# A new order of work at the two attention-to-MLP joints of a two-layer float32r transformer block

## The chip, the cores and the metric

One core of one Trainium2 chip runs the whole program. The metric is device time in microseconds. An engine name stands for: PE the matmul engine, DVE the vector engine, ACT the scalar engine, POOL the GpSimd engine, SP the engine that here only issues transfers. Each engine works through its own queue in order.

## The reference, cut to what matters

Batch 1, 256 latent tokens, 256 context tokens, width 1024, two layers. Layer 0 mixes latents and context by retention and passes both through an MLP; layer 1 lets the latents attend to a neighbourhood and to the context, and passes the latents alone through its MLP.

```python
for i in range(DEPTH):                      # DEPTH = 2
    h = x * (1.0 + sc1) + sh1
    hc = ctx * (1.0 + sc1c) + sh1c
    y, yc = mixer(h, hc, ...)               # retention (i = 0), neighbourhood attention (i = 1)
    x = layer_norm(ALPHA * x + g1 * y, ln_g[i, 0], ln_b[i, 0])
    h = x * (1.0 + sc2) + sh2
    x = layer_norm(ALPHA * x + g2 * sq_relu_mlp(h, w1[i], w2[i]), ln_g[i, 1], ln_b[i, 1])
    if not last:                            # the same for ctx with yc and the context's modulation
        ...
def sq_relu_mlp(h, w1, w2):
    return jnp.square(jax.nn.relu(h @ w1)) @ w2
```

A joint is the stretch between the last products of a mixer's output projection and the first products of the MLP: residual add, layer norm, transposition, modulation, and then `h @ w1`.

## The kernel before

Every float32 operand of a product is split in two float32r parts: `hi` is ACT's cast of it, `lo` is DVE's (or POOL's) subtraction of `hi` from it. A product a*b is three matmuls: ah*bh, ah*bl, al*bh. A weight tile comes by one transfer of 512 KB into one of four `raw` buffers; `fetch` issues the transfer and ACT's cast to `hi` and puts the subtraction on a list; `lows(n)` runs the first n of that list; `take(n, ahead, open_)` fetches and subtracts until enough units are there and hands out n of them (`open_` units may still lack their `lo`). `hi` and `lo` have five buffers each; a `raw` buffer is free again when its `lo` is made, so a late `lo` is a late transfer four units further on.

A scheduler puts all instructions into the engines' queues by their order in the program and by when it reckons their operands ready. An engine wrapper with `.on = True` pins an instruction behind the one traced just before it on that engine; instructions that aren't pinned may still be put ahead of pinned ones.

Layer 0's joint. Four token tiles t of 128 (0 and 1 are latents, 2 and 3 context). `proj` makes a tile's output projection, `add_to` adds it to the residual `R`, `stat` and `moments` give mean and `rstd` (the power is POOL's), `shift_of` makes `nmr`, `white` is the normalized tile `xn`, `turn` transposes it on PE into two PSUM tiles `pt`, `affine` modulates these to `aff` (half 0 on DVE, half 1 on ACT), `mod_split` makes `hTh` (ACT) and `hTl`. The MLP's first weight columns come in units of 512 x 256; two units make a pair, called `us[0:2]` and `us[2:4]` for the first two pairs. `mm1` multiplies a pair by the columns `LAT` (256 latents, matmuls 256 wide), `CTX` (256 context columns) or `ALL` (512 wide) into two PSUM banks; both column ranges of a pair share the banks. `evac1` takes a bank out by `relu_sq`: Relu on ACT, the square `r<-p,r` on DVE, a cast on ACT, a subtraction on DVE. The latents' products of the two pairs run while tiles 2 and 3 are made ready; the context's products follow, once the latents' part of the same bank is out.

Layer 1's joint. Two latent tiles. Output-projection weights come in eight units; the last two for half 1 lie in a slot (`hilo`) and in scratch tiles (two 512-column pieces). `attend(n)` ends with `rt`, `oTh`, `oTl` of head group n. `settle_last` adds a half of a tile to `R`, `center` makes `x0` and `x1`, `mod_pt` turns them (`pts0`, `pts1`), `affine_half` modulates tile 0, `direct` tile 1, `tok_part` are the first MLP products in token-major form, `turn_block` transposes their activations into `hid`. `settle_quarter` adds tile 1's second half in two quarters. The opening is the first pass of the loop over `f4`, `f2` that follows: `f4 == 1 and f2 == 0`. I number the MLP's weight units of this layer u0, u1, ...: each `f2` uses two of them (the opening u4 and u5, the next u6 and u7, then u8 and u9, and so on).

PE, ACT and DVE are pinned through both joints; POOL is pinned in the second half of layer 1's; SP is not pinned.

Of the kernel before, what the change touches and what calls it, by code (L numbers as in the profile page):

```python
# [10 lines left out]
F32 = mybir.dt.float32  # L11
F32R = mybir.dt.float32r
AF = mybir.ActivationFunctionType
# [91 lines left out]
def kernel(  # L105
# [171 lines left out]
    def lows(n=100):  # L277
        for lo, raw, hi in pending[:n]:
            dve.tensor_sub(out=lo, in0=raw, in1=hi.bitcast(F32))
        del pending[:n]  # L280
# [366 lines left out]
    def mod_split(tmp, half, t, eng, halves=False):  # L647
        ks = slice(4 * half, 4 * half + 4)
        if halves:
            hi, lo = (  # L650
                h[:, ks, :NLAT].rearrange("p k (b r) -> p k b r", b=2)[:, :, :, 64 * t : 64 * t + 64]
                for h in (hTh, hTl)
            )
            split(tmp[:].rearrange("p (k b r) -> p k b r", k=4, b=2), hi, lo, eng)
            return
        split(tmp[:].rearrange("p (k t) -> p k t", k=4), hTh[:, ks, tsl(t)], hTl[:, ks, tsl(t)], eng)

# [412 lines left out]
    for h in range(RH):  # L1070
# [159 lines left out]
        else:  # L1230
# [14 lines left out]
            def white(t, mv, r):  # L1245
                act.activation(out=xns[t], in_=R[t], func=AF.Identity, scale=r[:], bias=shift_of(mv, r)[:])
# [4 lines left out]
            def affine(t, pts):  # L1251
                return [mod_aff(pts[half], half, t, A, B) for half in range(2)]
# [12 lines left out]
            white(0, *m0)  # L1265
# [8 lines left out]
            white(1, *m1)  # L1274
# [12 lines left out]
            white(2, *m2)  # L1287
# [27 lines left out]

    G2 = None
    for hf in range(2):
# [9 lines left out]
        if hf == 0:  # L1327
            us = take(2, 2)
            pbs = [[bank("p1") for _ in range(2)] for _ in range(2)]
            hts = [hslot(fp) for fp in range(2)]  # L1330
            mm1(us, LAT, pbs[0], range(0, 4))
            take(0, 1)
            f2 = affine(2, turn(2))
            white(3, *m3)
            mm1(us, LAT, pbs[0], range(4, KC))
            us += take(2, 2)
            for half in range(2):
                mod_split(f2[half], half, 2, dve)
            mm1(us[2:4], LAT, pbs[1], range(0, 4))
            p3 = turn(3)  # L1340
            mm1(us[2:4], LAT, pbs[1], range(4, KC))
            f3 = affine(3, p3)
            take(0, 1)
            for half in range(2):
                mod_split(f3[half], half, 3, dve)
            for fp in range(2):
                evac1(pbs[fp], LAT, hts[fp])
            for e in ORDER:
                e.on = False
            for fp in range(2):  # L1350
                mm1(us[2 * fp : 2 * fp + 2], CTX, pbs[fp])
                evac1(pbs[fp], CTX, hts[fp])
            hid += hts
            outside()
# [532 lines left out]
    add_to(1, 0, t01[0], dve)  # L1887
    invert(n)
    gather(n)
    attend(n - 1)  # L1890
    flip(n)
    turned(n)
    lows(1)
    fetch(1, at=N_V)
    lows(1)
    fetch(1, True)

    us = take(4, 0, 2)
# [7 lines left out]
    def wo_last(t, half, cols=slice(0, 512)):  # L1906
        ps = wops[half, t, cols.start] if half else bank("pnw")
        mmo(ps, t, (4, 5, 6, 7), us[2 * half : 2 * half + 2], cols, start=half == 0)
        return ps
# [32 lines left out]
    fetch(1)  # L1942
# [9 lines left out]
    us4 = take(2, 0)  # L1952
# [65 lines left out]
    lo0 = [affine_half(pts0, half, 0, True, (dve, pool)[half]) for half in range(2)]  # L2018
# [3 lines left out]
    lo0[0]()  # L2022
# [5 lines left out]
    lo0[1]()  # L2028
# [194 lines left out]
```

## Time and profile before

| what | us |
|---|---|
| median of 3 runs | 1208.73 (1206.9 to 1209.21) |
| the profiled execution | 1205.15 |
| its span, first to last instruction | 1203.4 |
| layer 0's joint in the span | about 436 to 484 |
| layer 1's joint in the span | about 986 to 1056 |

All instructions issued through the wrappers carry one line (L84) in the profile, so a group is known by its names: `lo<-raw,hi` is a weight's subtraction, `hi<-raw` its cast, `hTl<-aff,hTh` a tile's low part. In a row of the timeline the columns are start, length (of the whole group, where `xN` tells of N alike), engine, line, operation, output and inputs, shape, count; a bracket tells how long the engine sat idle before it and what ended that.

### The profile page before, as it was taken

What the parts mean: (1) busy time and instruction counts of PE and PEld (TensorE: products, weight loads), DVE (VectorE), ACT (ScalarE), POOL (GpSimd) and SP (SyncE); (2) the same over time, 40 slices, a digit from 0 to 9 for tenths busy, and PEclk for the clock granted to TensorE, in tenths of its full rate; (3) what the DMA queues carried; (4) which work ended last, traced back from release to release, by engine and by line L of the source; (5) the groups of instructions that cost most, each with busy time, mean ns of one, the idle gap of its engine ahead of it and who ended that gap; (6) DMA issues with size and microseconds to landing.
All of it is one profiled execution on the core that took longest, in us unless ns stands there. A gap on an engine that the chain in (4) does not pass through costs nothing.

```text
span 1203.4 us, 17830 instructions
## 1 busy us (share of the span) xinstructions
PE 1176.1 (98%) x6867; PEld 986.4 (82%) x6867; DVE 825.5 (69%) x1307; ACT 477.8 (40%) x809; POOL 255.0 (21%) x390
## 2 busy tenths in 40 slices
PE   7999899999999999999999999999999999999997
PEld 5777788788878888888888888889778878999886
DVE  3778676768576478667876675578576688787445
ACT  3562122323222246442122333227466665666341
POOL 1103400420340131491203000122444431000001
PEclk9999999999999999999999999999999999999999
DMA  9766443344143123856566655546244335566660
GB/s 302 225 228 193 144 134 107 105 133 165 62 154 117 59 82 117 263 113 195 170 197 204 211 189 196 185 150 204 80 144 133 103 115 162 182 211 202 236 210 36
DMA packets 130265, 193.16 MB, mean 161 GB/s; under 512 B 9676, under 2 KB 73332, under 8 KB 130180
## 3 DMA queue, kind: packets, MB, share of 16 engines
q1 hardware_dynamic: 121796, 179.02, 46.1%
q0 software_dynamic: 7232, 10.44, 3.9%
q10 hardware_dynamic: 1152, 2.56, 0.7%
q8 instruction: 54, 0.88, 0.3%
q14 instruction: 31, 0.25, 0.1%
HBM read 187.15 MB, written 5.75 MB: 160 GB/s over the span
## 4 chain that ended last, share of the span: by engine, by line
PE 82%; DVE 8%; DMA 4%; issue 2%; ACT 2%; POOL 1%; SPq 0%; DVEq 0%; ACTq 0%; POOLq 0%
PE p L84 40%; PE pq L84 7%; PE pv L84 7%; PE pn L84 5%; PE pg L84 5%; PE pw L84 4%; PE pnv L84 4%; DMA rawa<-in_ada_w_dram 2%; DVE lo L84 2%; PE po L84 2%; PE ppt L84 2%; PE pS L84 1%; PE pqk L84 1%; PE pada L84 1%; PE pav L84 1%
## 5 line engine op out<-in xcount | busy, mean ns | idle before, releaser
L84 ACT CAST hi<-raw 128x1024 fp32r<-128x1024 f32 (+2 forms) x228 | 231.9, 1032 | 323.6 <-PE p L84 123.4
L84 DVE TENSOR_TENSOR lo<-raw,hi 128x1024 fp32r<-128x1024 f32 (+2 forms) x228 | 274.0, 1214 | 109.5 <-ACT hi L84 109.1
L84 PE MATMUL p<-hi,hid 128*128 128x512 f32 (+1 forms) x832 | 241.8, 374 | 0.0
L84 PEld LDWEIGHTS p<-hi,hid 128*128 128x128 f32 x832 | 152.2, 188 | 27.7
L84 PE MATMUL p<-hTh,lo 128*128 128x256 f32 (+1 forms) x512 | 167.5, 327 | 1.9 <-DVE lo L84 1.9
L84 PE MATMUL p<-hTh,hi 128*128 128x256 f32 (+1 forms) x512 | 167.9, 328 | 0.2 <-ACT hTh L84 0.2
L84 PE MATMUL p<-hTl,hi 128*128 128x256 f32 (+1 forms) x512 | 167.3, 327 | 0.4 <-DVE hTl L84 0.4
L84 PE MATMUL p<-lo,hid 128*128 128x512 f32 (+1 forms) x416 | 155.3, 373 | 0.0
L84 DVE SCALAR_TENSOR_TENSOR acc<-rawa,scol,acc 128x1024 f32<-128x1024 f32 x56 | 74.7, 1344 | 66.0 <-DMA rawa<-in_ada_w_dram 66.0
L84 POOL TENSOR_TENSOR R<-R,acc 128x512 f32<-128x512 f32 x40 | 63.2, 1596 | 209.9 <-DVE acc L84 209.8
L84 PEld LDWEIGHTS p<-hTh,lo 128*128 128x128 f32 x512 | 96.4, 188 | 11.2 <-DVE lo L84 2.5
L84 PEld LDWEIGHTS p<-hTl,hi 128*128 128x128 f32 x512 | 96.4, 188 | 9.5 <-DVE hTl L84 0.8
L84 PEld LDWEIGHTS p<-hTh,hi 128*128 128x128 f32 x512 | 96.3, 188 | 9.2 <-ACT hTh L84 0.4
L84 PEld LDWEIGHTS p<-lo,hid 128*128 128x128 f32 x416 | 78.4, 188 | 13.6
L84 ACT CAST hid<-r 128x256 fp32r<-128x256 f32 (+1 forms) x64 | 32.0, 500 | 109.9 <-DVE r L84 109.9
L84 DVE SCALAR_TENSOR_TENSOR strips<-rawa,scol,strips 128x512 f32<-128x512 f32 x84 | 66.8, 830 | 9.8 <-DMA rawa<-in_ada_w_dram 9.7
L84 POOL TENSOR_TENSOR rstd<-rstd,misc 128x1 f32<-128x1 f32 x28 | 18.8, 672 | 208.5 <-DVE rstd L84 207.2
L84 PE MATMUL pw<-hi,ol 128*128 128x512 f32 x128 | 51.0, 398 | 6.5 <-DVE ol L84 6.5
L84 ACT ACTIVATE s<-s,mn 128x512 f32<-128x512 f32 x64 | 45.5, 713 | 26.2 <-DVE mn L84 26.2
L84 PE MATMUL pw<-hi,oh 128*128 128x512 f32 x128 | 51.6, 403 | 0.0
L84 PE MATMUL pg<-hi,hTh 128*128 128x512 f32 x128 | 51.3, 401 | 0.0
L84 PE MATMUL pw<-lo,oh 128*128 128x512 f32 x128 | 50.5, 394 | 0.0
(238 smaller groups left out, 2288.3 us busy)
## 6 DMA issues: line engine op xcount, KB each, us to landing
raw<-in_mlp_w_dram SPq DMA_DIRECT2D x128, 512.0 KB, 4.5
rawa<-in_ada_w_dram SPq DMA_DIRECT2D x80, 512.0 KB, 3.9
raw<-in_ret_w_in_dram SPq DMA_DIRECT2D x42, 512.0 KB, 3.5
raw<-in_nat_w_in_dram SPq DMA_DIRECT2D x24, 512.0 KB, 5.1
rawq<-in_ada_w_dram SPq DMA_DIRECT2D x16, 512.0 KB, 6.4
raw<-in_ret_w_o_dram SPq DMA_DIRECT2D x16, 512.0 KB, 3.5
bias<-rpb_rows POOLq DMA_DIRECT2D x32, 128.0 KB, 2.9
raw<-in_nat_w_o_dram SPq DMA_DIRECT2D x8, 512.0 KB, 4.2
```

The costliest lines, as they stand in the source:

```text
L84: r = f(*args, **kwargs)
```

## The change

Layer 0's joint. One more weight unit is fetched ahead of tile 2's `white`. The shift of tile 3 is made ahead of tile 2's `affine`, and tile 3's `white` stands between the casts of tile 2's halves. The low parts of a tile are separated from its casts (`mod_high` returns the subtraction, to be run later), half 1 first. The context's products run in a new function `ctx_mm1`: all high-by-high products of both banks first, then the two others, and k from 4 to 7 ahead of 0 to 3; PE stays pinned through them.

Layer 1's joint. `invert` of the last head group moves behind `attend` of the one before, the residual's add of t01 behind `flip`; the scratch unit is fetched behind the last `attend`, one of its two subtractions goes to POOL; tile (0, half 1)'s products run as `wo_parts`, the products with the weights' low parts last; one MLP unit is fetched two steps earlier; both low parts of tile 0 go to POOL (one was DVE's); the first products of the second hidden block are split in two; in the opening, a fetch and its subtraction follow each of the two evacuations, and the transposed activations go between them.

```diff
+    def mod_high(tmp, half, t):
+        ...
+        act.copy(out=hi, in_=raw)
+        return lambda: dve.tensor_sub(out=lo, in0=raw, in1=hi.bitcast(F32))
...
             take(0, 2)
-            white(2, *m2)
+            fetch(1)
+            white(2, shift_of(*m2), m2[1])
...
+    def ctx_mm1(us, pb):
+        for i in range(2):
+            for k in (4, 5, 6, 7, 0, 1, 2, 3):
+                pe.matmul(
+                    pb[i][:, CTX], lhsT=us[k // 4][0][:, k % 4, tsl(i)], rhs=hTh[:, k, CTX],
+                    start=k == 4, stop=False,
+                )
+        for i in range(2):
+            for k in (4, 5, 6, 7, 0, 1, 2, 3):
+                wh, wl = (w[:, k % 4, tsl(i)] for w in us[k // 4])
+                pe.matmul(pb[i][:, CTX], lhsT=wl, rhs=hTh[:, k, CTX], start=False, stop=False)
+                pe.matmul(pb[i][:, CTX], lhsT=wh, rhs=hTl[:, k, CTX], start=False, stop=k == 3)
...
-            us = take(2, 2)
+            us = take(2, 2, 1)
...
             mm1(us, LAT, pbs[0], range(0, 4))
-            take(0, 1)
+            lows(1)
+            shift = shift_of(*m3)
             f2 = affine(2, turn(2))
-            white(3, *m3)
+            fetch(1)
+            low21 = mod_high(f2[1], 1, 2)
+            white(3, shift, m3[1])
+            low20 = mod_high(f2[0], 0, 2)
             mm1(us, LAT, pbs[0], range(4, KC))
+            lows(1)
+            low21()
             us += take(2, 2)
-            for half in range(2):
-                mod_split(f2[half], half, 2, dve)
             mm1(us[2:4], LAT, pbs[1], range(0, 4))
             p3 = turn(3)
             mm1(us[2:4], LAT, pbs[1], range(4, KC))
             f3 = affine(3, p3)
+            low20()
+            low31, low30 = (mod_high(f3[half], half, 3) for half in (1, 0))
+            low31()
+            low30()
             take(0, 1)
-            for half in range(2):
-                mod_split(f3[half], half, 3, dve)
             for fp in range(2):
                 evac1(pbs[fp], LAT, hts[fp])
-            for e in ORDER:
+            for e in ORDER[1:]:
                 e.on = False
             for fp in range(2):
-                mm1(us[2 * fp : 2 * fp + 2], CTX, pbs[fp])
+                ctx_mm1(us[2 * fp : 2 * fp + 2], pbs[fp])
                 evac1(pbs[fp], CTX, hts[fp])
+            pe.on = False
...
     wo_first(1, 0)
-    add_to(1, 0, t01[0], dve)
-    invert(n)
     gather(n)
     attend(n - 1)
+    invert(n)
     flip(n)
     turned(n)
     lows(1)
+    add_to(1, 0, t01[0], dve)
     fetch(1, at=N_V)
-    lows(1)
-    fetch(1, True)
-
-    us = take(4, 0, 2)
+    us = take(2, 0)
...
     attend(n)
+    lows(1)
+    fetch(1, True)
     mmo(ps, 0, (6, 7), us[0:2], start=False, k0=4)
-    lows(2)
+    lows(1, pool)
+    lows(1)
+    us += take(2, 0)
+    settle_last(0, 0, ps)
     fetch(1)
-    settle_last(0, 0, ps)
     lows(1)
-    settle_last(0, 1, wo_last(0, 1))
+    settle_last(0, 1, wo_parts(0, 1))
     mv0, r0 = moments(0)
     wo_first(1, 1, HALVES)
+    fetch(1)
...
-    fetch(1)
+    us4 = take(2, 0, 1)
     lows(1)
     settle_last(1, 0, wo_last(1, 0))
...
-    lo0 = [affine_half(pts0, half, 0, True, (dve, pool)[half]) for half in range(2)]
+    lo0 = [affine_half(pts0, half, 0, True, pool) for half in range(2)]
+    for low in lo0:
+        low()
     ps = [wo_last(1, 1, cols) for cols in HALVES]
     for q in range(2):
         stat_quarter1(q)
-    lo0[0]()
     settle_quarter(2, ps[0])
     settle_quarter(3, ps[1])
...
-    lo0[1]()
...
     tok_part(p00, 0, 0, *HL, LOW)
+    tok_part(p00, 0, 0, *LH, LOW)
     tok_part(p00, 0, 0, *HH, HIGH)
     tok_part(p00, 0, 0, *HL, HIGH)
-    tok_part(p00, 0, 0, *LH, LOW)
-    tok_part(p01, 0, 1, *HH, start=True)
+    tok_part(p01, 0, 1, *HH, LOW, start=True)
     tok_part(p01, 0, 1, *LH, LOW)
     tok_part(p00, 0, 0, *LH, HIGH, stop=True)
+    tok_part(p01, 0, 1, *HH, HIGH)
...
             mm1(us, LAT, pb, at=AT)
-            if opening:
-                turn_block(r10, 1, 0)
-                turn_block(r11, 1, 1)
-                for e in (pe, act, dve, pool):
-                    e.on = False
             dve.on = f4 < 3
             for i in range(2):
                 relu_sq(pb[i], LAT, ht[:, 2 * f2 + i, 0, :], ht[:, 2 * f2 + i, 1, :])
+                if opening:
+                    fetch(1)
+                    lows(1)
+                if opening and i == 0:
+                    turn_block(r10, 1, 0, hid[0])
+                    turn_block(r11, 1, 1, hid[0])
+            if opening:
+                for e in (pe, act, pool):
+                    e.on = False
```

`wo_parts(t, half)` runs the twelve matmuls of `wo_last` for k = 4 to 7, first those with the weights' `hi`, then those with their `lo`.

More of the change, by code (lines that the diff above doesn't have):

```diff
@@ L275, in fetch, with lows @@
             units.append((hi, lo))
-    def lows(n=100):
+    def lows(n=100, eng=None):
         for lo, raw, hi in pending[:n]:
-            dve.tensor_sub(out=lo, in0=raw, in1=hi.bitcast(F32))
+            (eng or dve).tensor_sub(out=lo, in0=raw, in1=hi.bitcast(F32))
         del pending[:n]
@@ L656, in mod_split @@
         split(tmp[:].rearrange("p (k t) -> p k t", k=4), hTh[:, ks, tsl(t)], hTl[:, ks, tsl(t)], eng)
+    def mod_high(tmp, half, t):
+        ks = slice(4 * half, 4 * half + 4)
+        raw, hi, lo = tmp[:].rearrange("p (k t) -> p k t", k=4), hTh[:, ks, tsl(t)], hTl[:, ks, tsl(t)]
+        act.copy(out=hi, in_=raw)
+        return lambda: dve.tensor_sub(out=lo, in0=raw, in1=hi.bitcast(F32))
     def modulate(src, t, A, B):
@@ L1243, in proj, with white @@
                 return gated(tok_mm(t, half, wus[half]), t, half, G1)
-            def white(t, mv, r):
-                act.activation(out=xns[t], in_=R[t], func=AF.Identity, scale=r[:], bias=shift_of(mv, r)[:])
+            def white(t, shift, r):
+                act.activation(out=xns[t], in_=R[t], func=AF.Identity, scale=r[:], bias=shift[:])
             def turn(t):
@@ L1264 @@
             add_to(1, 0, proj(1, 0), pool)
-            white(0, *m0)
+            white(0, shift_of(*m0), m0[1])
             tmp = proj(1, 1)
@@ L1273 @@
             add_to(2, 0, proj(2, 0), pool)
-            white(1, *m1)
+            white(1, shift_of(*m1), m1[1])
             for half in (1, 0):
@@ L1908, in wo_last, with wo_parts @@
         mmo(ps, t, (4, 5, 6, 7), us[2 * half : 2 * half + 2], cols, start=half == 0)
+        return ps
+    def wo_parts(t, half):
+        oTh, oTl = oTs[0]
+        ps = wops[half, t, 0]
+        for parts in (((0, 0), (1, 0)), ((0, 1),)):
+            for k in (4, 5, 6, 7):
+                w = us[2 * half + (k - 4) // 2]
+                for a, b in parts:
+                    pe.matmul(
+                        ps[:], lhsT=(oTh, oTl)[a][:, k, tsl(t)], rhs=w[b][:, k % 2, :],
+                        start=False, stop=k == 7 and b == 1,
+                    )
         return ps
@@ L1951 @@
     ht = slot(N_Q, [P, 4, 2, NLAT], F32R, "hid1")
-    us4 = take(2, 0)
     def toks(t):
```

## The prediction

> **What bounds the kernel now.** I read the page first (which engine is full), then the table of stages, then the list of PE's waits, then the timelines of PE, DVE, ACT and POOL in the two joints.
>
> ```profile
> span 1203.4 us, 17830 instructions
> PE 1176.1 (98%) x6867; PEld 986.4 (82%) x6867; DVE 825.5 (69%) x1307; ACT 477.8 (40%) x809; POOL 255.0 (21%) x390
> ...
> 600.00:700.00 100.00, 100.00 (x449) 82.28 (x448) 70.33 (x74) 27.52 (x36) 9.73 (x9) 1.00 0.63 199
> ...
> PE pw L84 <- DVE ol L84: 6.5, 4, 2.8
> ```
>
> PE is busy 98% of the span, in the open stretch of the MLP all of it (the stage row). No product is added or removed, so the change can only move PE's waits, and those are few. The largest entry, 6.5 us of `ol`, is of products in layer 0's heads, which the change doesn't touch. The joints hold these:
>
> ```profile
> 466.69 0.39 PE L84 MATMUL p<-hTh,lo 128*128 128x256 f32 x1 [0.76 <-DVE lo L84]
> ...
> 469.82 0.73 PE L84 MATMUL p<-hTh,hi 128*128 128x512 f32 x2 [0.23 <-ACT hTh L84]
> 470.90 0.50 PE L84 MATMUL p<-hTl,hi 128*128 128x512 f32 x1 [0.35 <-DVE hTl L84]
> ...
> 471.94 0.39 PE L84 MATMUL p<-hTh,lo 128*128 128x512 f32 x1
> 472.17 0.28 PE L84 MATMUL p<-hTh,hi 128*128 128x256 f32 x1
> ...
> 1001.05 0.51 PE L84 MATMUL pnw<-hi,oTh 128*128 128x512 f32 x1 [0.56 <-ACT oTh L84]
> 1010.22 1.04 PE L84 MATMUL pt<-cst,xn 128*128 128x128 f32 x8
> 1019.41 1.09 PE L84 MATMUL pt<-cst,xn 128*128 128x128 f32 x8 [0.64 <-DVE xn L84]
> 1040.64 0.39 PE L84 MATMUL p<-hTh,lo 128*128 128x256 f32 x1 [0.49 <-DVE lo L84]
> 1053.82 0.39 PE L84 MATMUL p<-hTh,lo 128*128 128x256 f32 x1 [0.66 <-DVE lo L84]
> ```
>
> A 512-wide product lasts 0.39 but the next starts 0.23 later (471.94 to 472.17), so records overlap by 0.16 and a wait costs its bracket plus 0.16. Layer 0: 0.92 + 0.39 + 0.51 = 1.82 us. Layer 1: 0.72 + 0.80 + 0.65 + 0.82 = 2.99. Together 4.8 us, the most that can be won here. Also note 469.82 to 472.17: seven 512-wide products of the third weight pair, put ahead of the first 256-wide context product at 472.17.
>
> **Layer 0's joint, step by step.**
>
> ```profile
> 460.54 1.23 DVE L84 TENSOR_TENSOR lo<-raw,hi 128x1024 fp32r<-128x1024 f32 x1
> 461.68 1.36 DVE L84 TENSOR_SCALAR aff<-pt,AB 128x128 f32<-128x128 f32 x4
> 465.41 1.23 DVE L84 TENSOR_TENSOR lo<-raw,hi 128x1024 fp32r<-128x1024 f32 x1 [2.25 <-ACT hi L84]
> 466.55 1.29 DVE L84 TENSOR_TENSOR hTl<-aff,hTh 128x512 fp32r<-128x512 f32 x2
> 469.03 1.22 DVE L84 TENSOR_TENSOR lo<-raw,hi 128x1024 fp32r<-128x1024 f32 x1
> 471.37 0.42 DVE L84 SCALAR_TENSOR_TENSOR r<-p,r 128x256 f32<-128x256 f32 x1
> ...
> 465.28 1.13 ACT L84 CAST hTh<-aff 128x512 fp32r<-128x512 f32 x2
> 466.32 1.49 ACT L84 ACTIVATE aff<-pt,AB 128x128 f32<-128x128 f32 x4
> ...
> 460.76 1.42 POOL L84 TENSOR_TENSOR rstd<-rstd,misc 128x1 f32<-128x1 f32 x1 [2.32 <-DVE rstd L84]
> ```
>
> Tile 3's shift now goes ahead of tile 2's four DVE modulations (1.36). It is bound by POOL's power, done at 460.76 + 1.42 = 462.2, so it gains about 0.7 us; the cover is lost for the modulations, which slip by as much, but nobody on PE waits for tile 2 yet. The next weight's cast no longer stands behind tile 3's `white`; its `lo` comes behind the modulations, near 463.6 to 464.9 instead of 465.41 to 466.63. PE wants it at 465.8: the 0.92 goes. The transposes of tile 3 stay where they are, since PE reaches them in its own order; ACT, freed of the two casts at 465.28, starts tile 3's modulation at 465.7 instead of 466.32 and DVE as early instead of 467.75.
>
> Then tile 3 is cast (two of 0.57) by 468.3, its low parts are done by 469.1. Behind them stand, as before, the third pair's cast (1.05, ACT) by 469.2 and its `lo` by 470.4, and only behind that the evacuation of the latents, whose first `r<-p,r` ends near 470.8 instead of 471.79. That matters: the first context product starts at 472.17, right behind the `r<-p,r` that ends at 471.79, because it writes the bank that this reads. PE, with 0.92 saved, ends the latents at about 468.5 and so has 2.3 us to the evacuation; the high products of both banks come first, so the second bank's evacuation, 1.2 later, adds 0.25. The pins order the context's products behind the latents', but the third pair's products aren't pinned and can be put ahead again: they need only that pair's cast (469.2). They fill 1.6 of the gap, and PE loses 0.7 to 1.1 instead of 1.82. I take **0.75 gained**; if nothing fills the gap it is 2.55 lost, 0.75 worse than before. The rest of the edits here (half 1 first, k from 4) only makes the order of use fit the order of arrival.
>
> **Layer 1's joint, up to the second tile's transposes.**
>
> ```profile
> 999.25 1.22 DVE L84 TENSOR_TENSOR hilo<-raw,hilo 128x1024 fp32r<-128x1024 f32 x1
> 1000.39 0.28 DVE L84 TENSOR_TENSOR rt<-pav,rt 128x128 f32<-128x128 f32 x1
> 1001.24 1.28 DVE L84 TENSOR_TENSOR lo<-raw,hi 128x512 fp32r<-128x512 f32 x2
> 1002.45 0.68 DVE L84 TENSOR_TENSOR acc<-pnw,G 128x512 f32<-128x512 f32 x1
> 1003.16 0.69 DVE L84 TENSOR_TENSOR R<-R,acc 128x512 f32<-128x512 f32 x1
> ...
> 457.13 1.30 POOL L84 TENSOR_TENSOR R<-R,acc 128x512 f32<-128x512 f32 x1 [2.15 <-DVE acc L84]
> 457.69 1.29 DVE L84 TENSOR_TENSOR R<-R,acc 128x512 f32<-128x512 f32 x1
> ...
> 224.63 3.84 POOL L84 TENSOR_TENSOR gs<-sg,gs 128x512 f32<-128x512 f32 x2 [7.30 <-ACT sg L84]
> 227.24 2.31 DVE L84 TENSOR_TENSOR lo<-raw,hi 128x1024 fp32r<-128x1024 f32 x1
> ```
>
> `rt` of the last head group now stands ahead of hilo's 1.22: it comes at about 999.4 instead of 1000.39 and PE's 0.72 goes. But DVE, not PE, sets when tile 0 is normalized: its rows above follow each other with no gap but the one of 0.36 behind `rt` (1000.67 to 1001.24, with `oTl` in it). On its queue the residual's add (0.69) comes into this stretch, and one scratch subtraction (0.64) leaves for POOL. POOL is no free hand here. At 457 us a DVE add, 0.69 alone (1003.16), took 1.29: it ended 0.55 behind POOL's pass, which began first. At 227 a DVE subtraction, 1.22 alone, took 2.31: POOL's two passes, 1.30 each alone, end at 228.47 and it had to wait for the one already queued. Such passes, all with two operands in SBUF, exclude each other, and the one that waits gets the next turn. So: hilo's subtraction runs behind `oTl`, 1000.25 to 1001.46; POOL's pass, ready at 1000.5, waits and ends at 1002.65; DVE's half waits for that and ends at 1003.2. `acc` starts at 1003.1 instead of 1002.45, **0.65 later**, and all behind it to x0 too.
>
> The Trainium skill has this as a rule (SBUF — State Buffer, section "Who interferes with whom"): a DVE instruction with two SBUF inputs and a GpSimd instruction that reads SBUF contend for one port pair, held for the whole instruction, and the other fully blocks. The rows at 457 agree (1.29 for 0.69). By it this joint gives nothing; were the move to POOL free it would be the second rival below.
>
> ```profile
> 1009.13 0.82 ACT L84 ACTIVATE xn<-R,nmr,rstd 128x512 f32<-128x512 f32 x1 [7.17 <-DVE nmr L84]
> ...
> 1015.21 1.59 POOL L84 TENSOR_TENSOR hTl<-aff,hTh 128x512 fp32r<-128x512 f32 x1 [6.37 <-ACT hTh L84]
> ...
> 1016.46 0.62 DVE L84 TENSOR_TENSOR R<-R,acc 128x256 f32<-128x256 f32 x1
> ```
>
> x0's ACT half is done at 1009.95 + 0.65 = 1010.6. PE, 0.72 ahead, is at `pts0` near 1009.5 and now stands there 1.1: it starts at 1010.63 instead of 1010.22. ACT's modulation follows 0.4 later, so POOL's second low part runs from 1015.6 instead of 1015.21, alone 1.30, to 1016.9. The add of the last quarter, which ended at 1017.08, has to wait for it and ends near 1017.2; the earlier `lo` of u1 and the missing subtraction of half 0 on DVE win nothing, since POOL's two passes hold DVE's two quarter adds. x1 follows as before: `pts1` at about 1019.5 for 1019.41. The 0.80 stays in another place. This joint: **0.1 lost**, with bounds of 1.0 lost (each of POOL's three passes at 1.59, the row at 1015.21, for 1.30) and 1.8 gained (all of x0 and x1 ahead, no blocking).
>
> **The opening of layer 1's MLP.**
>
> ```profile
> 1031.75 1.05 ACT L84 CAST hi<-raw 128x1024 fp32r<-128x1024 f32 x1
> 1035.53 0.76 DVE L84 TENSOR_TENSOR hid<-pt,hid 128x256 fp32r<-128x256 f32 x2 [2.82 <-ACT hid L84]
> 1039.36 3.49 DVE L84 TENSOR_TENSOR lo<-raw,hi 128x1024 fp32r<-128x1024 f32 x3
> ...
> 1040.64 0.37 SPq L84 DMA_DIRECT2D raw<-in_mlp_w_dram  x1
> ...
> 1045.81 1.06 ACT L84 CAST hi<-raw 128x1024 fp32r<-128x1024 f32 x1 [2.19 <-DMA raw<-in_mlp_w_dram]
> ```
>
> u8 is cast by 1032.8, DVE then sits idle for 2.82, yet u8's `lo` waits to 1039.36, pinned behind the transposed activations and both evacuations. PE waits for it (0.65). Its `raw` is free only then, so the transfer of u12 is issued at 1040.64, ACT stands 2.19 for it at 1045.81 in front of evacuations, these come late on DVE, and PE's 0.82 at 1053.82 is the end of that chain. With the fetch and subtraction behind the first evacuation, `lo` of u8 falls near 1034.6 to 1035.8, u12's transfer 5 us earlier. Both waits go: **1.47 gained**; at worst the second stays, 0.65.
>
> **The sum.** 0.75 - 0.1 + 1.47 = 2.1 us: the profiled execution of 1205.15 (span 1203.4 and 1.75 around it) would become 1203.0. The median of the runs is 3.6 above that execution; the same step from it gives **1206.6**. About 0.2% (2.4 us) is what this kernel's measurement tells from no change, so the forecast is a small gain at the edge of that.
>
> **The rivals.** (A) Nothing fills the wait for the evacuation in layer 0: -0.75 in place of +0.75, in all 0.6 gained, 1208.1. For it: PE is now pinned there. Against it: the third pair isn't, and at 469.82 it was put ahead. (B) POOL's passes don't hold DVE: x0 and x1 come early enough that PE waits only about 0.4 at `pts0`; 0.75 + 1.8 + 1.47 = 4.0, so 1204.7. Against it: the rows at 457 and 227; for it: much of DVE's work there reads PSUM, as the `acc` row. (C) Slower: the order in the open stretch, laid anew from 480 on, gets waits where it has none. The place would be a `lo` or `hTl` behind other DVE work; the price is the longest of its kind, 2.8 (the wait for `ol`); it decides from 2.1 on. One gives 1209.4, two 1212.2. Against it stands the stage that is busy 100.00 of 100. (D) The opening's order doesn't do it, DVE's early `lo` pushing the evacuations instead: 0.65 gained in all, 1208.1.
>
> **How the numbers follow.** Forecast 0.42, with its own range 1205.3 to 1208.1 from the bounds of its terms; A 0.17, B 0.18, C 0.15, D 0.08. Faster by over 0.2%: most of B and not quite half of the forecast, 0.36. Slower by over 0.2%: C and a tail of A, 0.17. Within: 0.47. The range reaches down to B with the runs' own spread of 1.2, and up past C's first wait: 1203.5 to 1210.2.
>
> **What would show it.** Right: no wait for `lo` right behind tile 3's transposes in layer 0, and a shorter one for `r<-p,r` with 512-wide products in it; around 1001 no wait for `oTh`, but one for `xn` at the first transposes; POOL's passes and DVE's adds longer than 1.30 and 0.69 beside each other; no wait for `lo` at u8 and u12. Wrong: `pts0` earlier than now (B), PE idle over 2 us ahead of the context's products (A), a stage after 480 below 100 (C).

## The result, and the profile after

| | before | after |
|---|---|---|
| median of 9 runs each, side by side | 1207.58 (1206.28 to 1209.48) | 1204.48 (1202.27 to 1205.08) |
| the profiled execution | 1205.15 | 1203.91 |

The ratio is 0.9971 (95% interval 0.9962 to 0.9980): a gain of about 3.1 us, where 2.1 were forecast (1206.6 for 1208.73, a ratio of 0.9982, which lies just above the interval). The page after, its span and its busy shares:

```profile
span 1202.1 us, 17829 instructions
...
PE 1174.6 (98%) x6867; PEld 985.5 (82%) x6867; DVE 827.7 (69%) x1305; ACT 478.5 (40%) x809; POOL 258.7 (22%) x392
```

The timeline of PE after, in the two joints (start, length of the group, engine, line, operation, names, shape, count, idle time before it and what ended that):

```profile
469.15 0.28 PE L84 MATMUL p<-hTh,lo 128*128 128x256 f32 x1
470.29 0.50 PE L84 MATMUL p<-hTh,hi 128*128 128x512 f32 x1 [0.85 <-ACT hi L84]
...
471.55 0.50 PE L84 MATMUL p<-hTh,lo 128*128 128x512 f32 x1
471.89 1.35 PE L84 MATMUL p<-hTh,hi 128*128 128x512 f32 x9
...
1011.12 1.09 PE L84 MATMUL pt<-cst,xn 128*128 128x128 f32 x8 [1.25 <-ACT xn L84]
...
1020.04 1.09 PE L84 MATMUL pt<-cst,xn 128*128 128x128 f32 x8 [0.87 <-DVE xn L84]
```

Layer 0 has lost its wait for `lo`. What is left is 0.85 + 0.16 = 1.01 us for the cast of the third weight pair, and 0.23 more inside the products that follow; six of that pair's products fill the time to 472.12, where the context's first product starts (the row at 471.89 begins with the sixth of them, 0.23 long). In layer 1 the wait for `oTh` is gone, and 1.41 us (1.25 + 0.16) now stand in front of the first transposes and 1.03 in front of the second. No wait for `lo` follows anywhere in the opening.

DVE and POOL after, same view:

```profile
470.27 1.23 DVE L84 TENSOR_TENSOR lo<-raw,hi 128x1024 fp32r<-128x1024 f32 x1 [0.17 <-ACT hi L84]
471.41 0.42 DVE L84 SCALAR_TENSOR_TENSOR r<-p,r 128x256 f32<-128x256 f32 x1
...
1000.73 1.22 DVE L84 TENSOR_TENSOR hilo<-raw,hilo 128x1024 fp32r<-128x1024 f32 x1
1001.87 1.78 DVE L84 TENSOR_TENSOR lo<-raw,hi 128x512 fp32r<-128x512 f32 x1
1003.57 0.68 DVE L84 TENSOR_TENSOR acc<-pnw,G 128x512 f32<-128x512 f32 x1
...
1014.28 1.36 DVE L84 TENSOR_TENSOR R<-R,acc 128x256 f32<-128x256 f32 x1
...
1016.46 1.25 DVE L84 TENSOR_TENSOR R<-R,acc 128x256 f32<-128x256 f32 x1
...
1035.11 1.23 DVE L84 TENSOR_TENSOR lo<-raw,hi 128x1024 fp32r<-128x1024 f32 x1 [0.53 <-ACT hi L84]
```

```profile
1001.15 1.95 POOL L84 TENSOR_TENSOR lo<-raw,hi 128x512 fp32r<-128x512 f32 x1 [5.28 <-ACT hi L84]
...
1014.05 1.31 POOL L84 TENSOR_TENSOR hTl<-aff,hTh 128x512 fp32r<-128x512 f32 x1 [4.08 <-ACT hTh L84]
...
1016.11 1.32 POOL L84 TENSOR_TENSOR hTl<-aff,hTh 128x512 fp32r<-128x512 f32 x1 [0.75 <-ACT hTh L84]
```

Each of POOL's three passes has a DVE row beside it that is stretched: 1.78 where half of the pair took 0.64 before, and 1.36 and 1.25 where an add of 256 took 0.42. DVE's rows end 0.28 to 0.55 behind POOL's pass, less than one pass of their own. `lo` of u8 stands at 1035.11 instead of 1039.36.

To see where the time went, I take from each trace the starts of PE's products, subtract from each step (start to next start) the mean steady step of its shape in the trace of before, and add up the rest by stretch. This is PE's loss in us, with waits and slow pace together; below zero means steps a little under that mean. From 500 to 836 all kernels have 1.5 to 1.6; what stands ahead of 440 varies from execution to execution by more than 2 us and is left out.

| kernel | 440-500 | 836-984 | 984-1030 | 1030-1062 | 1062-end | sum with 500-836 |
|---|---|---|---|---|---|---|
| before | 3.07 | 28.04 | 7.96 | 0.93 | -0.79 | 40.8 |
| before, once more | 3.07 | 28.08 | 8.97 | 1.68 | -0.87 | 42.5 |
| after | 2.32 | 28.41 | 8.00 | -0.99 | -0.75 | 38.6 |
| after, once more | 2.30 | 28.41 | 8.00 | -0.83 | -0.75 | 38.7 |
| layer 0's joint alone | 2.30 | 28.49 | 8.66 | 1.02 | -0.88 | 41.1 |
| layer 1's joint alone | 3.05 | 28.04 | 8.27 | 1.14 | -0.82 | 41.2 |
| opening alone | 3.07 | 28.05 | 8.96 | -0.73 | -0.84 | 40.0 |
| third pair pinned | 5.03 | 28.03 | 8.43 | -0.92 | -0.83 | 41.3 |
| PE unpinned in layer 0 | 2.29 | 28.47 | 8.01 | -0.99 | -0.75 | 38.6 |
| scratch on DVE | 2.30 | 28.34 | 7.53 | 0.22 | 0.98 | 41.0 |
| low part 0 on DVE | 2.32 | 28.48 | 7.96 | -0.98 | -0.75 | 38.6 |
| quarters together | 2.29 | 28.43 | 6.95 | 0.22 | 0.99 | 40.4 |
| quarters and scratch | 2.32 | 28.35 | 6.97 | 0.22 | 0.97 | 40.4 |
| quarters, turns split | 2.32 | 28.46 | 6.90 | -0.86 | -0.71 | 37.7 |

With bounds at the same products instead of the same times the cells move by 0.15 at most, but for two: third pair pinned then has 28.41 and 7.96 in place of 28.03 and 8.43. The first two rows differ although they are one kernel. That is the first thing the experiments had to settle.

### The profile page after: what moved, and what is told of

It is laid out like the page before. It is cut to its first block, busy times and chain, and to the rows that moved or that the text cites. A ratio compares the mean times of both kernels' runs of the same rounds, so it can differ in the third digit from the quotient of the medians.

```text
span 1202.1 us, 17829 instructions
## 1 busy us (share of the span) xinstructions
PE 1174.6 (98%) x6867; PEld 985.5 (82%) x6867; DVE 827.7 (69%) x1305; ACT 478.5 (40%) x809; POOL 258.7 (22%) x392
## 4 chain that ended last, share of the span: by engine, by line
PE 86%; DVE 5%; DMA 4%; ACT 2%; POOL 1%; issue 1%; ACTq 0%; DVEq 0%; SPq 0%; POOLq 0%
PE p L84 43%; PE pq L84 7%; PE pv L84 7%; PE pg L84 6%; PE pw L84 5%; PE pn L84 5%; PE pnv L84 4%; PE po L84 2%; DMA rawa<-in_ada_w_dram 2%; PE pS L84 1%; PE ppt L84 1%; PE pqk L84 1%; PE pada L84 1%; DVE lo L84 1%; PE pav L84 1%
## 5 line engine op out<-in xcount | busy, mean ns | idle before, releaser
L84 ACT CAST hi<-raw 128x1024 fp32r<-128x1024 f32 (+2 forms) x228 | 232.1, 1032 | 322.4 <-PE p L84 117.8
L84 PE MATMUL p<-hTh,hi 128*128 128x256 f32 (+1 forms) x512 | 163.0, 328 | 0.9 <-ACT hi L84 0.9
```

The lines of the kernel that those rows point to most:

```text
L84: r = f(*args, **kwargs)
```

## The experiments

### The three parts, each alone

The change was cut in three: layer 0's joint; layer 1's joint up to the second tile's transposes; the opening. Each was put on the kernel before by itself (the diff above, its parts one at a time).

Layer 0's joint alone (`mod_high`, the new order of `shift_of`, `white` and the casts, `ctx_mm1`):

> Layer 0's joint as changed, everything from layer 1 on as before. The prediction's term is 0.75 us gained, so a ratio to before near 0.9994 and, by PE's rows, the wait of 0.92 for lo gone and one of about 0.8 in front of the context's products in its place. Rival A (nothing fills that wait) is 0.75 lost, 1.0006. A third theory, that the whole measured gain of 3.1 us comes from here because the order laid out behind 480 us comes out better too, says 0.9975 and shows as fewer waits behind 500 us.

Measured: ratio 0.9990 (0.9979 to 1.0002); PE's loss between 440 and 500 went from 3.07 to 2.30. The term is 0.77, by the same rows as in the whole change, and nothing moved between 500 and 836. Rival A and the third theory are out.

Layer 1's joint alone:

> Layer 1's joint up to the second tile's transposes as changed, layer 0 and the opening of the MLP as before. The prediction (POOL's passes and DVE's exclude each other) says no gain, 0.1 us lost, with first transposes some 0.4 us later against the products in front of them and a wait of about 1.1 there in place of the 0.56 for oTh. Rival B (POOL's passes cost DVE nothing) says 1.8 us gained, ratio 0.9985, with acc as early as before. The profile of the whole change has the first case's rows, so what this run tells is whether they stand without the other two parts.

Measured: ratio 1.0005 (0.9992 to 1.0019). Its rows are those of the whole change, POOL's pass 1.96, the adds 1.36 and 1.24, waits of 1.43 and 1.03 in front of the transposes; the joint's loss is 8.27 against the 7.96 of the first trace of before. No gain, as forecast; rival B is out.

The opening alone:

> Only the opening of layer 1's MLP as changed. The prediction says 1.47 us gained (ratio 0.9988) by both waits for lo gone, the one behind the fifth weight pair and the one 13 us later; rival D says that only the first goes, 0.65 gained. If the two waits of before have one cause (lo of u8 pinned late), both go here; if the second has to do with the rest of the change, it stays at about 0.8.

Measured: ratio 0.9998 (0.9981 to 1.0015). Both waits for `lo` are gone (0.93 to -0.73), so they had one cause, and rival D is out. (In the prediction D is that neither wait goes; its 0.65 is what the two other terms leave.) The interval holds the 0.9988 of the forecast as well as no gain at all, so the time decides nothing here. The ratios of the three parts add up to 0.9993, and the whole change has 0.9971. As their intervals reach 0.0011 to 0.0017 to either side, this is no contradiction, but what each part gives rests on its rows and not on its time.

In layer 1's joint, where every instruction and its order are those of before, this execution lost 1.0 us more than the first trace of before. Its timeline there, of DVE, POOL and PE:

```profile
1017.41 1.58 DVE L84 TENSOR_TENSOR R<-R,acc 128x256 f32<-128x256 f32 x1
...
1017.40 1.31 POOL L84 TENSOR_TENSOR hTl<-aff,hTh 128x512 fp32r<-128x512 f32 x1 [6.36 <-ACT hTh L84]
...
1022.57 1.09 PE L84 MATMUL pt<-cst,xn 128*128 128x128 f32 x8 [1.61 <-DVE xn L84]
```

In the trace of before the same pair stood at 1015.21 and 1015.21; POOL's pass took 1.59 (the row quoted in the prediction), the wait was 0.64, and the add was short:

```profile
1015.21 0.42 DVE L84 TENSOR_TENSOR R<-R,acc 128x256 f32<-128x256 f32 x1
```

Here POOL is 10 ns ahead: the add takes 1.58, POOL's pass 1.31, and PE waits 1.61.

### The kernel before, once more

> The kernel before once more, for its rows in layer 1's joint. In its first profile DVE's add of the third residual quarter and POOL's low part began together at 1015.21, the add took 0.42, and PE waited 0.80 before the second tile's transposes; with only layer 0's joint or only the opening changed, the same instructions in the same order stood 10 to 20 ns the other way round, the add took 1.57 and PE waited 1.77. Theory: it is a race, which either execution can lose, and the first profile showed the cheap side of it. This look then has an add of either 0.4 or 1.6, and a wait of 0.8 or 1.8 to match, nothing between. Rival: the kernel before always has the cheap side and the two parts, each by itself, brought the dear one; then this look shows 0.42 and 0.80 again. A dear one settles it for the race; a cheap one leaves both open.

The same stretch of this second execution of before:

```profile
1015.91 1.58 DVE L84 TENSOR_TENSOR R<-R,acc 128x256 f32<-128x256 f32 x1
...
1015.89 1.31 POOL L84 TENSOR_TENSOR hTl<-aff,hTh 128x512 fp32r<-128x512 f32 x1 [6.35 <-ACT hTh L84]
...
1021.07 1.09 PE L84 MATMUL pt<-cst,xn 128*128 128x128 f32 x8 [1.61 <-DVE xn L84]
```

The dear side, in the unchanged kernel: it is a race, and the first trace showed its cheap side. Of the four profiled executions that have this order (before twice, layer 0's part alone, the opening alone) three lost it. If DVE loses, its add takes 1.58 for 0.42, most of POOL's pass more; if POOL loses, its pass takes 1.59 for 1.31. With the conventions of the prediction PE's wait is 0.64 + 0.16 = 0.80 on the cheap side and 1.61 + 0.16 = 1.77 on the dear one, 0.97 apart. In this execution the two waits for `lo` were longer as well (1.26 and 1.06 by PE's steps, 0.65 and 0.82 in the first), so that the whole change saves 2.2 us against one execution of before and 3.9 against the other (the last column: 40.8 and 42.5 against 38.6). The measured 3.1 lies between.

The Trainium skill has the exclusion (SBUF — State Buffer, section "Who interferes with whom"): of a DVE and a GpSimd instruction that both need the shared pair, whoever issues first has it for the whole instruction. These rows agree, down to a lead of 10 to 20 ns.

### What fills layer 0's wait

```diff
             for fp in range(2):
                 ctx_mm1(us[2 * fp : 2 * fp + 2], pbs[fp])
                 evac1(pbs[fp], CTX, hts[fp])
-            pe.on = False
...
             mm1(us, ALL, pb)
+            if hf == 0 and fp == 2:
+                pe.on = False
```

> The whole change, but the third weight pair's products of layer 0 keep their place behind the context's, so that nothing can be put into PE's wait for the latents' evacuation. The prediction's account of layer 0 (a wait of some 2.3 us of which the seven products put ahead fill 1.6) says 1.4 to 1.6 us slower than the whole change, with a wait of about 2.3 in front of the first context product. The rival, that the evacuation is early enough by itself and the third pair's products were merely handy, says no difference (under 0.4 us).

Measured: ratio 1.0000 (0.9988 to 1.0012), and 5.03 us lost between 440 and 500 for 2.32. The row of the first context product in the timeline of PE, and the windows in front of it, behind it and after that (length, busy us of PE, PEld, DVE, ACT, POOL with counts, granted clock, DMA share, GB/s):

```profile
471.71 3.67 PE L84 MATMUL p<-hTh,hi 128*128 128x256 f32 x16 [2.45 <-DVE r L84]
```

```profile
468.99:471.70 2.71, 0.27 (x3) 0.07 (x1) 2.50 (x4) 1.36 (x4) 0.00 (x0) 1.00 0.07 19
471.70:475.10 3.40, 3.39 (x16) 3.39 (x17) 2.03 (x6) 2.06 (x6) 0.53 (x1) 0.50 0.52 154
475.10:479.00 3.90, 3.90 (x34) 3.90 (x34) 1.46 (x4) 1.59 (x4) 0.00 (x0) 1.00 0.00 0
```

The wait came, 2.45 us of idleness that cost 2.6 (2.45 + 0.16), and it took the clock with it: 0.50 for the next 3.4 us, in which 16 products ran that need 16 x 0.12 = 1.9 at full speed. Of the 2.7 us lost against the whole change (5.03 less 2.32), 3.4 - 1.9 = 1.5 is the clock; the remaining 1.2 is the filling. The fill is worth more than I said, since it also keeps the clock. By the Trainium skill (TensorE: Matmul & The Clock Gate, section "Part 1: The HAM clock gate (the "warmup" mystery)") the clock is halved after an idle window of about 3.4 us; here 2.45 us of idleness were enough.

The pin itself was taken away in another run:

```diff
-            for e in ORDER[1:]:
+            for e in ORDER:
                 e.on = False
             for fp in range(2):
                 ctx_mm1(us[2 * fp : 2 * fp + 2], pbs[fp])
                 evac1(pbs[fp], CTX, hts[fp])
-            pe.on = False
```

> The whole change, but PE isn't pinned for the context's products of layer 0 (the other engines aren't either, as before); their new order stays. If the pin is what lets the third pair's products into the wait for the evacuation, their count ahead of the first context product falls and the excess of PE between 440 and 500 us goes up from 2.2 to between 2.9 (as before) and 4.9 (nothing put ahead). If the casts and low parts that come earlier do it all, the excess stays at 2.2 and the pin is worth nothing.

```profile
470.39 0.50 PE L84 MATMUL p<-hTh,hi 128*128 128x512 f32 x1 [0.85 <-ACT hi L84]
...
471.98 1.34 PE L84 MATMUL p<-hTh,hi 128*128 128x512 f32 x9
```

Measured: ratio 0.9969 (0.9959 to 0.9979), loss 2.29. The scheduler finds the same six products for the gap and the same wait of 0.85. Pinning the context's products is worth nothing; the order of the casts, low parts and context products does it all.

### POOL as a helper of DVE

Both scratch subtractions back on DVE:

```diff
-    lows(1, pool)
-    lows(1)
+    lows(2)
```

> The whole change, but both scratch subtractions of the last projection weights stay on DVE. If POOL's pass and DVE's exclude each other, the move to POOL lengthened the chain that it was to shorten: DVE's half takes 0.64 in place of 1.78, both together 1.2, acc starts 0.4 to 0.5 us earlier against hilo's subtraction, the wait in front of the first tile's transposes falls from 1.41 to about 0.95 and the kernel gains some 0.45 us. If the move relieves DVE, taking it back costs 0.5 to 0.6 us: acc and that wait come later by that.

DVE and PE in this kernel:

```profile
999.91 1.22 DVE L84 TENSOR_TENSOR hilo<-raw,hilo 128x1024 fp32r<-128x1024 f32 x1
1001.04 1.29 DVE L84 TENSOR_TENSOR lo<-raw,hi 128x512 fp32r<-128x512 f32 x2
1002.25 0.69 DVE L84 TENSOR_TENSOR acc<-pnw,G 128x512 f32<-128x512 f32 x1
...
1009.80 1.09 PE L84 MATMUL pt<-cst,xn 128*128 128x128 f32 x8 [0.75 <-ACT xn L84]
```

From `hilo` to `acc` it is 1002.25 - 999.91 = 2.34 us, with POOL's help 1003.57 - 1000.73 = 2.84. The first transposes wait 0.91 (0.75 + 0.16) for 1.41, as expected: the move to POOL costs 0.5 us. Yet the ratio is 0.9987 (0.9975 to 0.9999), no better than the whole change's 0.9971: behind 1030 this trace loses 2.9 us more. That is the pace told of below.

The first tile's low part of half 0 back on DVE, as before:

```diff
-    lo0 = [affine_half(pts0, half, 0, True, pool) for half in range(2)]
-    for low in lo0:
-        low()
+    lo0 = [affine_half(pts0, half, 0, True, (dve, pool)[half]) for half in range(2)]
...
+    lo0[0]()
     settle_quarter(2, ps[0])
...
+    lo0[1]()
```

> The whole change, but the first tile's low parts as before: half 0 on DVE, half 1 on POOL. If the stretched adds (1.36 and 1.25 for 0.42 alone) are DVE waiting for POOL's pass, only the second stays: the first add takes 0.42, DVE has 0.67 more work of its own, the second add runs into POOL's pass and ends when that does, so the second tile's transposes come 0.0 to 0.2 us later than in the whole change; where the third quarter's add falls on POOL's pass instead it is the same sum. The move of half 0 to POOL is then worth nothing. If POOL is a free hand, giving 0.67 back to DVE costs 0.67.

```profile
1014.04 0.69 DVE L84 TENSOR_TENSOR hTl<-aff,hTh 128x512 fp32r<-128x512 f32 x1
...
1015.11 0.43 DVE L84 TENSOR_TENSOR R<-R,acc 128x256 f32<-128x256 f32 x1
...
1016.35 1.40 DVE L84 TENSOR_TENSOR R<-R,acc 128x256 f32<-128x256 f32 x1
```

The first add is short again, the second ends at 1017.75 (in the whole change at 1017.71), and the joint's loss is 7.96 for 8.00; ratio 0.9976 (0.9964 to 0.9989). Moving that half to POOL is worth nothing in this order. Against the kernel before, only the moment at which POOL begins has changed: 0.6 us after the first add has ended, so the race isn't open in this trace. In the whole change it isn't either, in another way: POOL leads both adds, by 0.23 and 0.35, and they lose every time (1.35 to 1.36, and 1.24 to 1.25, in all six profiles with that order).

### A joint with less waiting, and the pace behind it

Half of the second tile's last projection goes into PE's wait ahead of the first transposes, and DVE does both products from PSUM, both adds, both statistics:

```diff
+    ps = [wo_last(1, 1, HALVES[0])]
     pts0 = [mod_pt(x0, half) for half in range(2)]
...
-    ps = [wo_last(1, 1, cols) for cols in HALVES]
+    ps.append(wo_last(1, 1, HALVES[1]))
...
-    settle_quarter(2, ps[0])
-    settle_quarter(3, ps[1])
+    settle_quarters(ps)
```

> The whole change, and in layer 1's joint two orders more: PE does the first half of the second tile's last projection (12 products of 256, 1.44 us, whose operands are long there) ahead of the first tile's transposes, where it waits 1.41; DVE takes both PSUM products of the last two quarters first (0.41 each, which read one operand from PSUM), then both adds, then both statistics, so that one of POOL's passes holds up one add, not each pass one. Theory of the shared turn: the adds end 1.0 to 1.1 us earlier against the first transposes, the wait of 1.03 in front of the second tile's transposes shrinks or moves into the products in front of them, and the kernel gains 1.0 to 1.4 us on the whole change. If DVE's load by itself sets x1 and not the collisions, the adds end no earlier, and PE's 1.41 just comes up again at the second transposes: no gain.

DVE and PE in its joint:

```profile
1015.04 0.74 DVE L84 TENSOR_TENSOR acc<-pnw,G 128x256 f32<-128x256 f32 x2
1015.69 1.48 DVE L84 TENSOR_TENSOR R<-R,acc 128x256 f32<-128x256 f32 x2
...
1012.34 1.08 PE L84 MATMUL pt<-cst,xn 128*128 128x128 f32 x8
...
1020.23 1.03 PE L84 MATMUL pt<-cst,xn 128*128 128x128 f32 x8
```

Both adds together take 1.48 (1.36 + 1.25 in the whole change), neither group of transposes waits, and 7.9 us lie between the two (8.9 in the whole change). The joint's loss is 6.95, 1.05 less, as the theory of the shared turn says. But the ratio is 0.9996 (0.9981 to 1.0011). In the profiled execution the gain went here, in the windows from 1060 to 1100 of the whole change and of this kernel:

```profile
1060.00:1100.00 40.00, 40.00 (x355) 40.00 (x354) 29.74 (x47) 25.35 (x46) 0.00 (x0) 1.00 0.66 206
```

```profile
1060.00:1100.00 40.00, 40.00 (x342) 40.00 (x341) 29.11 (x45) 23.75 (x42) 0.00 (x0) 1.00 0.62 187
```

PE is busy all the time, at the same clock, with the same products in the same order, and does 355 in one and 342 in the other: 113.3 ns from start to start, or 117.8. It waits for nothing; the pace is there from the transposes near 1035 on and lasts to 1105, some 600 products, 2.8 us. Whether the other executions have it no trace shows: of the eleven runs eight lie at 1205.3 to 1209.1, the profiled one among them, and three at 1201.8 to 1203.4. Two runs asked whether the pace belongs to the kernel.

> The whole change once more, beside the next kernels on one chip. Two things are asked. First, whether the ratio of 0.9971 stands: with PE's waits 2.6 us shorter than in the first profile of before, and the lost race there (1.0 us) in most executions, 0.997 to 0.998 is expected. Second, the pace of the 256-wide products between 1040 and 1105 us: 113.3 ns each in the first profile of the change, 117.8 in two variants of it whose products come in nearly the same order and wait nowhere in this stretch. If the pace falls to one side or the other by chance at each resumption, this execution may show either; if it belongs to the kernel, it is 113.3 again. Either way the pace is worth some 2.8 us (620 products by 4.5 ns).

Measured: ratio 0.9975 (0.9966 to 0.9984), so the gain stands. 113.3 ns again, and the joint's rows to a few ns.

> The whole change with both of the orders that each took wait from layer 1's joint in its profile: quarters together (PE's excess there 1.0 us less than in the whole change) and scratch subtractions on DVE (0.5 less). If the two add up, the joint's excess is 1.2 to 1.5 less than in the whole change; if they remove the same wait, 1.0. The time follows only if the pace behind it is the same: 1.2 to 1.5 us faster than the whole change at 113.3 ns for a product, some 1.4 slower at 117.8.

Measured: ratio 0.9980 (0.9969 to 0.9991); the joint's loss 6.97, the same as with the quarters alone, so both edits remove the same wait; 117.8 ns, and a median 0.5 us over that of the whole change on the same chip (1204.45 and 1203.95; 1.4 was expected for the slow pace, if all runs had it).

The last variant keeps the quarters together and sets the opening's transposes one by one between its products, so that these are broken off more often:

```diff
     turn_block(r00, 0, 0)
-    turn_block(r01, 0, 1)
...
-            mm1(us, LAT, pb, at=AT)
+            if opening:
+                mm1(us, LAT, pb, range(0, 4), AT, (0,))
+                turn_block(r01, 0, 1, hid[0])
+                mm1(us, LAT, pb, range(4, KC), AT, (0,))
+                turn_block(r10, 1, 0, hid[0])
+                mm1(us, LAT, pb, range(KC), AT, (1,))
...
-                    turn_block(r10, 1, 0, hid[0])
```

> Quarters together as before (scratch on POOL), with one change behind it: the four pairs of 128-wide transposes of the opening, which stood two and two, stand singly among the 256-wide products of the fifth weight pair (behind none, 12, 24 and 48 of them). In the profiles so far the pace of these products was set anew at each such break: of six executions that came to the break near 1035 us at the slow pace of 117.8 three left it at 113.3, and all that came at 113.3 kept it. If each break is a draw of this kind, three breaks behind the first leave the slow pace in some 1 of 8, the profile shows 113.3 from 1040 on, and the gain of 1.0 us in the joint shows at last: ratio to before near 0.9965. If the pace follows from how the joint before it is ordered, it stays at 117.8 from 1040 to 1105 and the ratio near 0.9990. The breaks themselves cost some 0.1 us each.

The same windows of this kernel:

```profile
1060.00:1100.00 40.00, 40.00 (x356) 40.00 (x354) 29.12 (x45) 25.61 (x46) 0.00 (x0) 1.00 0.66 206
```

The profiled execution has the quick pace and the least loss of all, 37.7; it took 1202.72, against 1203.91 for the first profile of the change. But the ratio over the runs is 0.9983 (0.9974 to 0.9992), median 1205.29, and the eleven runs reach from 1202.7 to 1206.5. The interval leaves out the 0.9965 of the one theory and just holds the 0.9990 of the other. One execution at the quick pace shows that this order can have it; that the breaks bring it in seven of eight is not borne out. Within it the steps behind the four breaks settle at 113, 118, 118 and 113 ns: a break can take the quick pace away as well. Nothing tried here beats the change over its runs beyond the intervals.

## Why the prediction was right, and where a term was off

**Layer 0.** 0.75 was forecast, 0.75 came (3.07 to 2.32; alone 0.77). The wait for `lo` went, and the gap in front of the context's products was filled by the third pair. The times of the prediction are on the clock of the first trace; the trace of after stands 0.92 later here, by tile 3's transposes (465.53 for 464.61). On the first one's clock the third pair's cast ended at 469.3 (469.2 was forecast), the evacuation's first `r<-p,r` at 470.9 (470.8), and PE was through with the latents at 468.35 (468.5). So every step came within 0.15 us, but the differences add up in PE's wait: 1.01 and 0.23, together 1.24, for the 0.7 to 1.1 forecast. The term still came out at 0.75, for it had gone by the dear end of that range (1.82 - 1.1 = 0.72), and other steps in the stretch gave back 0.17. Rival A's condition, when forced, came as described, with a wait of 2.6; its price was too low, 2.7 rather than 1.5, for want of the clock.

**Layer 1, up to the second transposes.** The steps came as written: no wait for `oTh`, POOL's passes and DVE's rows excluding each other, no gain against the first trace of before (8.00 for 7.96; 0.1 lost was forecast). The trace of after stands 0.57 later where the joint begins (984.74 for 984.17, the same product); less that, `acc` starts at 1003.00 (1003.1 was forecast), `pts0` at 1010.55 (1010.63) and `pts1` at 1019.47 (1019.5). Only the wait at `pts0` was longer, 1.41 for 1.1. Rival B fell with these rows. What was off is the size of the term's other side: "the 0.80 stays in another place". The 0.80 was one outcome of a race, read off two rows that begin at the same 1015.21. The other outcome is 1.77, and three of four executions of that order had it. Against the one of them that is before itself the term is 1.0 gained (8.97 to 8.00), not 0.1 lost. Two rows of engines that exclude each other and that start within 10 to 20 ns are a cost with two values; the row of 1.59 for a pass that takes 1.31 alone already told of the collision.

**The opening.** 1.47 was forecast, and both waits went, from one cause, as the opening alone shows. The stretch gained more, 1.92 (0.93 to -0.99). Some 0.2 of the rest is a cost of a wait that the prediction's bracket plus 0.16 leaves out: the product that has waited is followed by the next 0.22 later (1040.64 to 1040.86) instead of 0.113. About another 0.2 is pace: 47 products near 1030 ran at 117.9 ns in the first trace of before and at 114.0 in that of after. The waits vary too: 1.47 in the first execution of before, 2.32 in the second.

**The sum.** 2.1 forecast; 2.2 against the first trace of before, 3.9 against the second, 3.1 in the median. That 2.2 meets 2.1 is in part luck: the opening gave 0.45 more than its term, and between 836 and 984 the change loses 0.37 that the prediction put at nothing. That loss is in one group of twelve products of 32 rows. DVE, the weight loads (PEld) and PE there, first before, then after:

```profile
901.31 0.69 DVE L84 TENSOR_TENSOR kT<-pn,kT 128x512 fp32r<-128x512 f32 x1 [1.64 <-ACT kT L84]
...
902.00 0.58 PEld L84 LDWEIGHTS pqk<-kT,qT 32*128 32x128 f32 x12 [0.20 <-DVE kT L84]
902.00 1.01 PE L84 MATMUL pqk<-kT,qT 32*128 32x512 f32 x12
```

```profile
894.68 0.23 DVE L84 COPY rr<-sums 128x128 f32<-128x128 f32 x1 [0.48 <-DVE sums L84]
...
901.89 0.69 DVE L84 TENSOR_TENSOR kT<-pn,kT 128x512 fp32r<-128x512 f32 x1 [1.64 <-ACT kT L84]
...
902.21 1.39 PE L84 MATMUL pqk<-kT,qT 32*128 32x512 f32 x12
...
902.64 0.53 PEld L84 LDWEIGHTS pqk<-kT,qT 32*128 32x128 f32 x9 [0.17 <-DVE kT L84]
```

Before, DVE's low part `kT` is made (902.00) when PE comes to these products; after, it is made at 902.58, behind the third weight load, and the fourth follows at 902.64. The fourth product starts 0.43 behind the first, where it was 0.05, which is the loss. PE's own row shows no bracket, since the wait is the weight load's. `kT` is late by the idleness of 0.48 in front of `rr` 7 us earlier: from there on DVE's and ACT's rows stand 0.57 later than in the first trace of before, and PE's 0.21. The ten profiles with layer 0's part of the change all have that idleness, and the group takes 1.26 to 1.34 from its first start to the next group's; the four without that part have no such idleness, and 0.90 to 0.96. So it comes with the order of layer 0's part; what the copy of `rr` waits for stays open, as the instruction on `sums` that the bracket names had ended 0.48 before.

Rival C had the right sort of place, a low part behind other work in a stretch made anew, and this is a case of it, at 0.37 and not at 2.8: nothing between 500 and 836 moved, and from 1062 on the change is as before. Beside it, a stretch with no waits at all can run 4% slower, and three variants of the joint did so.

## What to carry to other kernels

Where the passes of two engines exclude each other, look for rows that begin together: such a pair has two prices, and one trace shows one of them, so profile the kernel before a second time before taking a term from it. Before comparing times of two traces, take off what they stand apart ahead of the stretch. Handing DVE's work to POOL bought nothing here wherever both work on operands in SBUF; keeping the scratch subtractions on DVE (0.5 us less wait), or doing the rows that read PSUM while POOL runs (1.05 us less loss in the joint), did shorten the joint, though not the time over the runs. And after an edit count the products in the untouched stretch behind it: a gain in a joint of 1 us can be paid back by a pace that is 4% slower for 70 us.

## What the runs showed of the hardware that was not expected

- A 256-wide product at the full granted clock has two steady paces, 113.3 and 117.8 ns, in the same order of the same instructions. Of the six profiled executions that came to the break near 1035 us (four transposes) at the slow pace three left it at the quick one; of those that came at the quick one none went the other way there, but at an earlier break of the last variant one did (113 to 118 ns). The eight waits for `lo` tell nothing of this: PE came to all of them at the quick pace and left them at it. Each of the three variants that had the slow pace from 1035 to 1105 has a new order in the joint before it, but so have low part 0 on DVE and the turns split, which had the quick one. What chooses the pace is open; that it is worth 2.8 us here is shown.
- After 2.45 us without a product the clock went to 0.50 for 3.4 us, although PE had been busy all along before. The length of the idleness doesn't decide alone: near 120 us PE is idle for 1.85 us in the first execution of before and for 1.90 in the second, and only the second then has 0.50, for 3.4 us (512-wide products 427 ns apart instead of 227). The waits of 1.61 us at 1020 left the clock at 1.00.
- POOL's lead of 10 to 20 ns over DVE goes with 1.0 us more of PE's wait; where the rows show no lead (1015.21 for both), DVE came first.
